# Strassen-Winograd gate and up products: one trace order for all sets, with P4 cut into two halves

## The chip, the cores and the metric

The kernel runs on 1 core of one Trainium2 chip. The metric is the device time of one execution in microseconds (us), and the time of a kernel is the median of several executions. All values are float32; the products are made from float32r halves, as told below.

## The reference, cut to what matters

One step of a decoder layer for 512 prompt rows plus 8 sample rows, with a width of 2048. The part that the change touches is the first half of the SwiGLU feed-forward layer: `silu(h1 @ w_gate) * (h1 @ w_up)`, with `h1` of 520 rows by 2048, and `w_gate` and `w_up` of 2048 by 5632. Before it come attention, pooling, an output projection and a layer norm; after it `w_down` and a second layer norm.

```
a = silu(einsum('btd,df->btf', h1, w_gate)) * einsum('btd,df->btf', h1, w_up)
ff = einsum('btf,fd->btd', a, w_down)
h = layer_norm(alpha*h1 + ff, ...)
```

## The kernel before, in words

**Tiling.** The 5632 output columns are 44 tiles of 128, taken as 22 pairs. For each pair there is a gate set `g<i>` and an up set `u<i>` (class `Set`), which run in turn: g0, u0, g1, u1, g2 and so on; pairs 5 and 16 come last. A set multiplies a 2x2 block of weights (two column tiles by two halves of the 2048 inputs) by a 2x2 block of activations (two halves of the inputs by two halves of 260 rows) by the Strassen-Winograd scheme: seven products P1 to P7 in place of eight.

**A product** (`prod`, line 969) takes 128x1024 weights: a raw block `q(r, c)` as loaded for P1, P2 and P4, or a sum of raw blocks, made by DVE on a 128x1024 tile (`weight_sum`, line 196), for P7, P6, P5 and P3. The sums chain: P7's goes into P6's, P6's overwrites the same block, and that goes into P5's and P3's. The weights are then split in two halves of 512 columns (`split`): ACT rounds them to float32r (`wh`, the CAST of line 187) and DVE subtracts to get the rest (`wl`, line 188). Each half feeds 12 matmuls of 128x260: four times `wh` by high part (L203), `wh` by low part (L204), `wl` by high part (L206). So a product is 24 matmuls.

**Rings.** `wh` and `wl` come from rings of `WB` = 5 slots, dealt out in the order in which the code is traced. The cast into a slot waits until the matmuls of the split five places earlier in the trace have read it. Raw blocks (512 KB each, loads of line 180 on SP's queue) lie in a ring of six, four blocks to a set.

**Banks.** Three PSUM banks per set: `al` (named `p1_...`) takes P1, P6, P5 and P3 in turn, accumulating, and between them the parts `c21`, `c22` are read out of it; `ga` (`p7_...`) takes P7 and, after its copy to `c22`, P4; `de` (`p2_...`) takes P2 alone. P5 may not write `al` until `c21` is read from it after P6 (line 1038, or line 1036 where P1 is filled in). P3 may not write it until `c22` is read from it after P5 (line 1050).

**Which sets have what.** g0 and u0 have P1 and P2 made ahead (`ahead`), so they run five products. Ten up sets (u1 to u4, u6 to u11) have P1 made ahead ("filled"): six products. All others run seven.

**The order.** `run` (line 1007) traces the products; the tile framework then schedules every engine's instructions by its own model, so a matmul may stand earlier or later than traced, as far as data, ring and bank allow. PE, ACT, DVE and SP each execute their list strictly in that order. Work that rides along: after each up set `staged` makes sums and splits of the result (lines 1097 to 1112) and stores them to `t_d`, pulled forward by `next(side)` in the next gate set.

Of the kernel before, what the change touches and what calls it, by code (L numbers as in the profile page):

```python
# [67 lines left out]
def hybrid_step(ctx, tc, xin, w_in, w_o, w_g, w_u, w_d, w_pool, par_d, cst_d, ident_d, ln2gb, kct_d, vc_d, hist_d,  # L68
# [83 lines left out]
    def row_tile(name, w=NTOK):  # L152

        return ap_.tile([P, NTOK], F32, tag="row", name=name, bufs=bufs["row"])[:, :w]
# [28 lines left out]
    def split(s, name, lo=None):  # L183

        wh, wl = [sp[0].tile(list(s.shape), F32R, tag=t, bufs=sp[1]) for t in ("wh", "wl")]
        with tc.high_priority(prio[0]):
            nc.scalar.copy(wh, s)  # L187
            last_lo[0] = (lo or nc.vector).tensor_sub(wl, s, wh.bitcast(F32)).ins  # L188
        return wh, wl
# [10 lines left out]
    def products(out, wh, wl, hi, lo, first, last, onto=False):  # L200

        for j, o in enumerate(out):
            nc.tensor.matmul(o, wh, hi[j], start=first, stop=False, skip_group_check=onto)  # L203
            nc.tensor.matmul(o, wh, lo[j], start=False, stop=False, skip_group_check=onto)  # L204
        for j, o in enumerate(out):
            nc.tensor.matmul(o, wl, hi[j], start=False, stop=last, skip_group_check=onto)  # L206
# [48 lines left out]
    with ExitStack() as sa:  # L255
# [185 lines left out]
        for h in range(2):  # L441
            for g in range(4):
                n = h * 4 + g + 1
# [244 lines left out]
        def sample_attention():  # L688
# [10 lines left out]
            nc.scalar.copy(sT.rearrange("p j n -> p (j n)"), st_.rearrange("p j t b -> p (j t b)"))  # L699
            prod = pa.tile([P, 8, NS], F32, tag="smp", name="prod")  # L700
            nc.vector.tensor_add(prod, qd[:, 0], qd[:, 1])
            for i in range(2):
                ts = slice(4 * i, 4 * i + 4)
# [111 lines left out]
    def bank(name, w=HN):  # L815
        return ps.tile([P, 512], F32, tag="bank", name=name, bufs=banks)[:, :w]
# [130 lines left out]
    class Set:  # L947
# [18 lines left out]
            self.s((1, 0), (0, 0), (1, 0), nc.vector.tensor_sub)  # L966
            self.s3 = True

        def prod(self, n, bk, first=True):


            b = {1: "b11", 2: "b21", 3: "b22", 4: "t4", 5: "t1", 6: "t2", 7: "t3"}[n]
            src = {1: lambda: self.q(0, 0), 2: lambda: self.q(0, 1), 4: lambda: self.q(1, 1),
                   7: lambda: self.q(1, 0) if self.s3 else self.s((1, 0), (0, 0), (1, 0), nc.vector.tensor_sub),
                   6: lambda: self.s((1, 0), (1, 1), (1, 0), nc.vector.tensor_sub),
                   5: lambda: self.s((0, 0), (1, 0), (0, 0), nc.vector.tensor_add),
                   3: lambda: self.s((0, 1), (0, 1), (1, 0), nc.vector.tensor_sub)}[n]()
            for g in range(2):
                wh, wl = split(src[:, g * 512:(g + 1) * 512], f"{self.name}_{n}{g}")
                if g == 0 and n == 1:  # L980
                    self.early()
                if g == 0 and n == 3 and self.next and (self.next.p1 is not None or self.next.bk):

                    self.next.early()
                for kk in range(4):
                    k = 4 * g + kk
                    sl = slice(kk * P, (kk + 1) * P)
                    hi, lo = bop[b][k // 2]
                    products([bk], wh[:, sl], wl[:, sl], [hi[:, k % 2, :]], [lo[:, k % 2, :]], k == 0 and first, k == 7, True)
# [17 lines left out]
        def run(self, c11, c12, c21, c22, side=(), out=None):  # L1007

            side = iter(side)
            r = row_tile(f"p_{self.name}")  # L1010
            filled = self.p1 is not None
            al, de = [self.bk.get(n) for n in (1, 2)]
            if not filled:
                self.p1 = r[:, HALF[0]]
                if al is None:
                    al = bank(f"p1_{self.name}")
                    self.prod(1, al)
                nc.scalar.copy(self.p1, al)
            else:
                al = bank(f"p1_{self.name}")  # L1020
            ga = bank(f"p7_{self.name}")
            next(side, None)
            self.prod(7, ga)
            next(side, None)
            kept = de is not None
            if filled and not kept:
                de = bank(f"p2_{self.name}")
                self.prod(2, de)
            if filled:
                nc.vector.tensor_add(c22, ga, self.p1)  # L1030
            else:
                nc.scalar.copy(c22, ga)
            self.prod(6, al, filled)
            next(side, None)
            if filled:
                nc.vector.tensor_add(c21, al, self.p1)
            else:
                nc.scalar.copy(c21, al)
            if filled or kept:
                self.prod(4, ga, False)  # L1040
            else:
                de = bank(f"p2_{self.name}")
                self.prod(2, de)
            next(side, None)
            nc.vector.tensor_add(c11, de, self.p1)
            if out:
                out(0)
            self.prod(5, al, False)
            next(side, None)
            nc.vector.tensor_add(c22, c22, al)  # L1050
            if not (filled or kept):
                self.prod(4, ga, False)
            next(side, None)
            nc.vector.tensor_add(c21, c21, ga)
            if out:
                out(1)
            self.prod(3, al, False)
            if filled:
                nc.vector.tensor_add(c12, al, self.p1)
                return c12  # L1060
            return al
# [68 lines left out]
    for j, s in enumerate(sets[NKEEP + 1::2][:NFILL]):  # L1130
        if j % 2 == 0:
            f = pb.tile([P, 2, HN], F32, tag="fill", name=f"fill{j}", bufs=NF)
# [82 lines left out]
    def column_pair(c, j):  # L1215

        A = {(r, b): wd[c, j, r, b] for r in range(2) for b in range(2)}
        tri = ps.tile([P, 3, 512], F32, tag="tri", name=f"tri{c}_{j}", bufs=2)[:, :, :HN]
        ga, de, al = [tri[:, i, :] for i in range(3)]
        ac = acc4[j]  # L1220
        if c == 0:
            for r in range(2):
                h = ac[:, 2 * r:2 * r + 2, :]
                nc.scalar.activation(h, h, AF.Copy, scale=ALPHA)

        def prod(n, bk, src, first=True):
            wh, wl = split(src, f"d{c}_{j}_{n}")
            for k in range(KP):
                hi, lo = ops[c][n][k][:, 0, :], ops[c][n][k][:, 1, :]
                products([bk], wh[:, k, :], wl[:, k, :], [hi], [lo], k == 0 and first, k == KP - 1, True)  # L1230

        def add(t, a, b, op):
            weight_sum(op, A[t], A[a], A[b])
            return A[t]


        prod(1, al, A[0, 0])
        yield
        prod(7, ga, add((1, 0), (0, 0), (1, 0), nc.vector.tensor_sub))
        nc.vector.tensor_add(ac[:, 1:3, :], ac[:, 1:3, :], tri[:, 0::2, :])  # L1240
        yield
        prod(2, de, A[0, 1])
        yield
        prod(6, al, add((1, 0), (1, 1), (1, 0), nc.vector.tensor_sub), False)
        nc.vector.tensor_add(ac[:, 0, :], ac[:, 0, :], al)
        yield
        prod(4, ga, A[1, 1], False)
        yield
        prod(5, al, add((0, 0), (1, 0), (0, 0), nc.vector.tensor_add), False)
        nc.vector.tensor_add(ac[:, 0:2, :], ac[:, 0:2, :], tri[:, 0::2, :])  # L1250
        yield
        prod(3, al, add((0, 1), (0, 1), (1, 0), nc.vector.tensor_sub), False)
        nc.vector.tensor_add(ac[:, 2:4, :], ac[:, 2:4, :], tri[:, 1:3, :])
        yield
# [9 lines left out]
    g, before = [column_pair(0, j) for j in range(2)]  # L1264
# [5 lines left out]
    for x, (c, j) in enumerate(pairs[2:], 2):  # L1270
        g = column_pair(c, j)
# [4 lines left out]
        for i in range(5):  # L1276
# [7 lines left out]
            elif j < 2 * len(PLAIN) and i == 0:  # L1284
# [3 lines left out]
                f = j  # L1288
# [233 lines left out]
```

## Time and profile before

| | |
|---|---|
| time, median of 3 | 1931.59 us (1929.88 to 1933.46) |
| span of the profiled execution | 1931.1 us, 0.5 under the median; its own time is not listed apart |
| PE busy (matmul) / PEld (weight load) | 1894.4 us (98%) / 1865.8 us (97%) |
| DVE busy / ACT busy | 1539.9 us (80%) / 944.1 us (49%) |
| DMA queue 1 | 315.71 MB, 49.7% of 16 engines |
| mean granted TensorE clock | 0.992 |

The gate and up sets run from about 590 to 1448 us of the span. In a timeline row the columns are start, duration, engine, line, operation, output and inputs, shapes, count; brackets at the end give the idle time just before, by the modelled end of the work before it, and what ended it.

### The profile page before, as it was taken

What the parts mean: (1) busy time and instruction counts of PE and PEld (TensorE: products, weight loads), DVE (VectorE), ACT (ScalarE), POOL (GpSimd) and SP (SyncE); (2) the same over time, 40 slices, a digit from 0 to 9 for tenths busy, and PEclk for the clock granted to TensorE, in tenths of its full rate; (3) what the DMA queues carried; (4) which work ended last, traced back from release to release, by engine and by line L of the source; (5) the groups of instructions that cost most, each with busy time, mean ns of one, the idle gap of its engine ahead of it and who ended that gap; (6) DMA issues with size and microseconds to landing.
All of it is one profiled execution on the core that took longest, in us unless ns stands there. A gap on an engine that the chain in (4) does not pass through costs nothing.

```text
span 1931.1 us, 39334 instructions
## 1 busy us (share of the span) xinstructions
PE 1894.4 (98%) x15533; PEld 1865.8 (97%) x15533; DVE 1539.9 (80%) x2734; ACT 944.1 (49%) x1808; POOL 2.7 (0%) x9
## 2 busy tenths in 40 slices
PE   9999999999999999999999999999999999999996
PEld 8999999999989999999999999999999999999996
DVE  6666667768777888888888888888877888888878
ACT  6644445545654544554455555555554444344341
POOL 0000000000000000000000000000000000000000
PEclk9999999999999999999999999999999999999998
DMA  8732222665744555454545445454469664645332
GB/s 276 233 101 66 71 78 75 211 202 193 250 150 164 160 160 172 142 162 158 175 139 178 141 138 165 146 167 145 164 212 356 214 221 162 223 163 202 94 99 89
DMA packets 145241, 319.28 MB, mean 165 GB/s; under 512 B 14288, under 2 KB 66232, under 8 KB 144952
## 3 DMA queue, kind: packets, MB, share of 16 engines
q1 hardware_dynamic: 144480, 315.71, 49.7%
q8 instruction: 122, 2.00, 0.4%
q10 hardware_dynamic: 576, 1.05, 0.2%
q14 instruction: 63, 0.52, 0.1%
HBM read 265.22 MB, written 54.03 MB: 165 GB/s over the span
## 4 chain that ended last, share of the span: by engine, by line
PE 92%; DVE 4%; ACT 2%; DMA 1%; issue 1%; SPq 0%; DVEq 0%; ACTq 0%
PE p_g L203 7%; PE p_g L204 7%; PE p_g L206 7%; PE p_u L203 7%; PE p_u L206 7%; PE p_u L204 7%; PE tri L203 7%; PE tri L206 7%; PE tri L204 7%; PE o L203 3%; PE o L206 3%; PE o L204 3%; PE p_u L996 2%; PE mm_u L203 2%; PE mm_u L206 2%; PE mm_u L204 2%
## 5 line engine op out<-in xcount | busy, mean ns | idle before, releaser
L187 ACT CAST rr<-fr 128x512 fp32r<-128x512 f32 (+1 forms) x1056 | 658.0, 643 | 776.6 <-DVE fr L196 224.0
L188 DVE TENSOR_TENSOR rr<-fr,rr 128x512 fp32r<-128x512 f32 (+1 forms) x1056 | 738.0, 717 | 264.5 <-ACT rr L187 253.2
L196 DVE TENSOR_TENSOR fr<-fr 128x1024 f32<-128x1024 f32 (+1 forms) x304 | 319.7, 1052 | 5.8 <-DMA fr<-in_w_g_dram 5.0
L203 PE MATMUL p_g<-rr 128*128 128x260 f32 x830 | 235.5, 285 | 7.4 <-ACT rr L187 7.1
L206 PE MATMUL p_g<-rr 128*128 128x260 f32 x830 | 230.6, 282 | 0.0
L204 PE MATMUL p_g<-rr 128*128 128x260 f32 x788 | 221.8, 282 | 0.0
L203 PE MATMUL p_u<-rr 128*128 128x260 f32 x770 | 217.5, 283 | 0.2 <-ACT rr L187 0.2
L206 PE MATMUL p_u<-rr 128*128 128x260 f32 x770 | 215.3, 282 | 0.0
L204 PE MATMUL p_u<-rr 128*128 128x260 f32 x748 | 210.6, 282 | 0.0
L206 PE MATMUL tri<-rr 128*128 128x260 f32 x696 | 196.8, 283 | 1.5 <-DVE rr L188 1.5
L203 PE MATMUL tri<-rr 128*128 128x260 f32 x696 | 197.0, 283 | 0.7 <-ACT rr L187 0.7
L204 PE MATMUL tri<-rr 128*128 128x260 f32 x696 | 196.7, 283 | 0.0
L203 PEld LDWEIGHTS p_g<-rr 128*128 128x128 f32 x830 | 156.2, 188 | 9.9 <-ACT rr L187 9.4
L206 PEld LDWEIGHTS p_g<-rr 128*128 128x128 f32 x830 | 155.2, 189 | 0.0
L204 PEld LDWEIGHTS p_g<-rr 128*128 128x128 f32 x788 | 148.1, 188 | 0.0
L203 PE MATMUL o<-rr 128*128 128x260 f32 x512 | 145.0, 284 | 0.3 <-ACT rr L187 0.3
L203 PEld LDWEIGHTS p_u<-rr 128*128 128x128 f32 x770 | 144.9, 188 | 0.3 <-ACT rr L187 0.3
L206 PEld LDWEIGHTS p_u<-rr 128*128 128x128 f32 x770 | 144.6, 189 | 0.0
L204 PE MATMUL o<-rr 128*128 128x260 f32 x512 | 144.1, 282 | 0.0
L206 PE MATMUL o<-rr 128*128 128x260 f32 x512 | 143.6, 282 | 0.2 <-DVE rr L188 0.2
L204 PEld LDWEIGHTS p_u<-rr 128*128 128x128 f32 x748 | 140.6, 188 | 0.0
L206 PEld LDWEIGHTS tri<-rr 128*128 128x128 f32 x696 | 131.3, 189 | 2.2 <-DVE rr L188 2.2
(320 smaller groups left out, 4570.0 us busy)
## 6 DMA issues: line engine op xcount, KB each, us to landing
fr<-in_w_u_dram SPq DMA_DIRECT2D x100, 512.0 KB
fr<-in_w_g_dram SPq DMA_DIRECT2D x90, 512.0 KB
fr<-in_w_d_dram SPq DMA_DIRECT2D x64, 640.0 KB
t_d<-fr SPq DMA_DIRECT2D x140, 260.0 KB
fr<-in_w_o_dram SPq DMA_DIRECT2D x64, 512.0 KB
fr<-in_w_in_dram SPq DMA_DIRECT2D x48, 512.0 KB
rr<-t_d SPq DMA_DIRECT2D x87, 260.0 KB
mid_b<-t_d SPq DMA_DIRECT2D x53, 260.0 KB
```

The source lines that it names most:

```text
L187: nc.scalar.copy(wh, s)
L188: last_lo[0] = (lo or nc.vector).tensor_sub(wl, s, wh.bitcast(F32)).ins
L196: i = op(*args).ins
L203: nc.tensor.matmul(o, wh, hi[j], start=first, stop=False, skip_group_check=onto)
L204: nc.tensor.matmul(o, wh, lo[j], start=False, stop=False, skip_group_check=onto)
L206: nc.tensor.matmul(o, wl, hi[j], start=False, stop=last, skip_group_check=onto)
L996: nc.tensor.matmul(bk, self.q(0, n - 1)[:, k * P:(k + 1) * P], z1[0][4 * (n - 1) + k // 2][:, k % 2, :], start=(k == 0), stop=(k == 7))
```

## The change

Before, the order of tracing depended on the set: P7, P2, P6, P4, P5, P3 where P1 is filled; P7, P6, P4, P5, P3 in g0 and u0; P1, P7, P6, P2, P5, P4, P3 in all others. Now each set traces [P1], P7, [P2], P6, first half of P4, P5, second half of P4, P3. With P4 in two traced halves, its two splits also take their ring slots at two places, before and behind P5's.

```diff
-        def prod(self, n, bk, first=True):
+        def prod(self, n, bk, first=True, halves=(0, 1)):
...
-            for g in range(2):
+            for g in halves:
                 wh, wl = split(src[:, g * 512:(g + 1) * 512], f"{self.name}_{n}{g}")
...
             next(side, None)
             self.prod(7, ga)
             next(side, None)
-            kept = de is not None
-            if filled and not kept:
+            if de is None:
                 de = bank(f"p2_{self.name}")
                 self.prod(2, de)
...
-            if filled or kept:
-                self.prod(4, ga, False)
-            else:
-                de = bank(f"p2_{self.name}")
-                self.prod(2, de)
+            self.prod(4, ga, False, (0,))
             next(side, None)
             nc.vector.tensor_add(c11, de, self.p1)
             if out:
                 out(0)
             self.prod(5, al, False)
             next(side, None)
             nc.vector.tensor_add(c22, c22, al)
-            if not (filled or kept):
-                self.prod(4, ga, False)
+            self.prod(4, ga, False, (1,))
             next(side, None)
             nc.vector.tensor_add(c21, c21, ga)
             if out:
                 out(1)
             self.prod(3, al, False)
```

Lines of the changed kernel that the orders below and the prediction name: 1040 is `c11` (1045 before), 1045 is `c22` (1050 before), 1048 is the sum into `c21` (1054 before), 1037 the copy of `c21` (1038 before), 1061 to 1063 the Silu of the gate (1067 to 1069 before), 1105 a staged cast (1111 before).

First place, PE's order in g6 where P6 ends, before (`p1_g6` is `al`, `p7_g6` is `ga`):

```order
L206 MATMUL p1_g6_8279<-rr_61 128x260
L203 MATMUL p1_g6_8279<-rr_61 128x260
L204 MATMUL p1_g6_8279<-rr_61 128x260
L206 MATMUL p1_g6_8279<-rr_61 128x260
L203 MATMUL p7_g6_8312<-rr_61 128x260 [waits Activation_49]
L204 MATMUL p7_g6_8312<-rr_61 128x260
L203 MATMUL p1_g6_8279<-rr_61 128x260 [waits Activation_49]
L204 MATMUL p1_g6_8279<-rr_61 128x260
L206 MATMUL p1_g6_8279<-rr_61 128x260 [waits DVE_49]
```

And now, PE's order in g6 at the end of the first half of P4:

```order
L204 MATMUL p7_g6_8312<-rr_61 128x260
L206 MATMUL p7_g6_8312<-rr_61 128x260
L203 MATMUL p7_g6_8312<-rr_61 128x260 [waits Activation_49]
L204 MATMUL p7_g6_8312<-rr_61 128x260
L203 MATMUL p1_g6_8279<-rr_61 128x260 [waits Activation_49]
L204 MATMUL p1_g6_8279<-rr_61 128x260
L206 MATMUL p1_g6_8279<-rr_61 128x260 [waits DVE_49]
```

Before, two matmuls of P4 followed the last of P6, and P5 followed them. Now twelve matmuls of P4, its whole first half, stand between P6 and the first pair of the second half, and P5 starts after that pair.

Second place, PE's order at the seam from g6 to the filled set u6, before:

```order
L204 MATMUL p7_g6_8312<-rr_61 128x260
L206 MATMUL p7_g6_8312<-rr_61 128x260
L203 MATMUL p7_u6_8518<-mid_b_3870,rr_61 128x260 [waits Activation_49]
L204 MATMUL p7_u6_8518<-mid_b_3870,rr_61 128x260
L203 MATMUL p1_g6_8279<-rr_61 128x260 [waits DVE_49]
```

And now:

```order
L204 MATMUL p7_g6_8312<-rr_61 128x260
L206 MATMUL p7_g6_8312<-rr_61 128x260
L203 MATMUL p7_u6_8518<-mid_b_3870,rr_61 128x260 [waits Activation_49]
L204 MATMUL p7_u6_8518<-mid_b_3870,rr_61 128x260
L203 MATMUL p2_u6_8547<-mid_b_3870,rr_61 128x260
L204 MATMUL p2_u6_8547<-mid_b_3870,rr_61 128x260
L203 MATMUL p1_g6_8279<-rr_61 128x260 [waits DVE_49]
```

A pair of u6's P2 has moved ahead of g6's P3, beside the pair of u6's P7 that stood there. In both, P4's last rows run just ahead of the seam.

Third place, ACT's order at the same seam, before (the cast that waits for DVE and PE is u6's P7, first half; the one behind it P7, second half; the one that waits for a DMA is u6's P2, first half):

```order
L187 CAST rr_61<-fr_60 128x512 [waits PE_49,Activation_49]
L187 CAST rr_61<-fr_60 128x512 [waits DVE_49,PE_49,Activation_49]
L187 CAST rr_61<-fr_60 128x512 [waits PE_49,Activation_49]
L187 CAST rr_61<-fr_60 128x512 [waits DMAHW3_49,PE_49]
L187 CAST rr_61<-fr_60 128x512 [waits PE_49,Activation_49]
```

And now (the cast that waits for a DMA and PE is u6's P2, first half; the two behind it are P7's halves):

```order
L187 CAST rr_61<-fr_60 128x512 [waits DVE_49,Activation_49]
L187 CAST rr_61<-fr_60 128x512 [waits PE_49,Activation_49]
L187 CAST rr_61<-fr_60 128x512 [waits DMAHW2_49,PE_49,Activation_49]
L187 CAST rr_61<-fr_60 128x512 [waits DVE_49]
L187 CAST rr_61<-fr_60 128x512
L1062 ACTIVATE fr_60<-fr_60 128x520 [waits DVE_49]
```

The cast of u6's P2 has moved ahead of both casts of u6's P7. In the trace's ring order P2's first half has the slot five places behind the second half of g6's P4.

## The prediction

> **What bounds the kernel now.** I read the page first, then the waits of PE, busy time by stretches, and the timelines of PE, ACT and DVE around PE's waits.
>
> ```profile
> PE 1894.4 (98%) x15533; PEld 1865.8 (97%) x15533; DVE 1539.9 (80%) x2734; ACT 944.1 (49%) x1808; POOL 2.7 (0%) x9
> ```
>
> PE is busy for 98% of the span, and the change keeps the number of its matmuls. So only waits of PE can move the time. Its waits, longest first:
>
> ```profile
> PE p_g L203 <- ACT rr L187: 7.1, 11, 0.6
> ...
> PE tri L203 <- DVE fr L1240: 0.8, 1, 0.8
> ...
> PE p_g L203 <- ACT fr L1038: 0.3, 1, 0.3
> ...
> PE p_u L203 <- ACT rr L187: 0.2, 1, 0.2
> ```
>
> Of these, the rows of `p_g` and `p_u` lie in the gate and up sets: twelve short waits for the cast of a weight half, and one for the copy of `c21`. By stretches (us, then PE, PEld, DVE, ACT, POOL, clock, DMA):
>
> ```profile
> 790.00:990.00 200.00, 196.62 (x1626) 195.41 (x1626) 172.53 (x279) 99.79 (x188) 0.00 (x0) 1.00 0.51 162
> 1190.00:1450.00 260.00, 259.26 (x2162) 259.05 (x2162) 216.40 (x332) 139.29 (x261) 0.00 (x0) 1.00 0.50 166
> ```
>
> The waits belong to the first half, where a seven-product gate set is followed by a filled up set. In the second, where all sets run seven products, PE hardly waits (0.74 of 260 us): there is nothing to win there. One wait in detail, on PE and then on ACT:
>
> ```profile
> 708.31 0.28 PE L203 MATMUL p_g<-rr 128*128 128x260 f32 x1
> 708.43 0.28 PE L204 MATMUL p_g<-rr 128*128 128x260 f32 x1
> 708.54 0.28 PE L206 MATMUL p_g<-rr 128*128 128x260 f32 x1
> 709.47 0.39 PE L203 MATMUL p_g<-rr 128*128 128x260 f32 x1 [0.64 <-ACT rr L187]
> 709.70 0.28 PE L204 MATMUL p_g<-rr 128*128 128x260 f32 x1
> 709.81 0.32 PE L203 MATMUL p_g<-rr 128*128 128x260 f32 x1
> 709.97 0.28 PE L204 MATMUL p_g<-rr 128*128 128x260 f32 x1
> ```
> ```profile
> 708.80 0.62 ACT L187 CAST rr<-fr 128x512 fp32r<-128x512 f32 x1 [0.81 <-PE p_g L204]
> 709.32 0.37 ACT L1038 COPY fr<-p_g 128x260 f32<-128x260 f32 x1
> 709.59 0.62 ACT L187 CAST rr<-fr 128x512 fp32r<-128x512 f32 x1
> ```
>
> Matmuls start 0.12 apart. The last L204 of P6 starts at 708.43; 0.37 later ACT, idle for 0.81 before, casts P4's first half, and 0.05 after that cast's end PE goes on. The cast waited for a slot: traced P6, P2, P5, P4, the first half of P4 is the fifth split behind the second half of P6, but PE runs P2 before P6 and a pair of P4 right behind P6. So P4's slot comes free only when its weights are due. The start gap is 0.93 in place of 0.12, and the next two uneven steps are 0.23 and 0.16: 0.81 + 0.11 + 0.04 = 0.96 us for a wait.
>
> **What goes.** Ten of the eleven waits of `p_g` are of this form. In the first, P5's pair waits once more, for the copy of `c21`:
>
> ```profile
> 631.31 0.28 PE L206 MATMUL p_g<-rr 128*128 128x260 f32 x1
> 632.23 0.39 PE L203 MATMUL p_g<-rr 128*128 128x260 f32 x1 [0.64 <-ACT rr L187]
> 632.46 0.28 PE L204 MATMUL p_g<-rr 128*128 128x260 f32 x1
> 633.04 0.39 PE L203 MATMUL p_g<-rr 128*128 128x260 f32 x1 [0.29 <-ACT fr L1038]
> 633.26 0.28 PE L204 MATMUL p_g<-rr 128*128 128x260 f32 x1
> ```
>
> From 631.31 to 633.26 are 1.95 us in place of four steps, 0.48: 1.47. Now P2 is traced before P6, as PE runs it, and twelve matmuls of P4 (1.44 us) lie between P6 and the next accumulation into `al`; the copy of 0.37 fits under them. Counting five splits back, P4's halves use slots that P7 and P6 left at least 25 matmuls (3 us) before. So all eleven should go: 10 x 0.96 + 1.47 = 11.1 us.
>
> **What comes.** At the seam to a filled up set (second and third place of the orders) PE ends P4's second half and goes to pairs of the next set's P7 and P2. P2's first half has the slot of P4's second half, whose last L204 runs one row before the seam, and ACT has that cast ahead of P7's. So the pair of P7, whose own weights are long summed, waits for two casts. What two take in a row, after a wait of the first:
>
> ```profile
> 833.38 1.14 ACT L187 CAST rr<-fr 128x512 fp32r<-128x512 f32 x2 [3.61 <-DMA fr<-in_w_u_dram]
> ```
>
> From the slot's last L204: 0.37 + 1.14 + 0.05 = 1.56 us to the pair, which would stand 0.24 behind that L204. That is 1.32, and with the uneven restart (0.11 + 0.04) 1.47 us. The orders show it at nine seams: those into u2 to u4 and u6 to u11, and not into u1. 9 x 1.47 = 13.2 us. P3, P2 and all that stands behind move by as much; nothing runs meanwhile on PE.
>
> One more comes at the end. In u16 no next set's P1 lies between P5 and P3, and P4's second half is scheduled ahead of P5, so P3 follows P5 at once and waits for `c22`. The nearest row is PE's wait for a DVE addition in the down stage:
>
> ```profile
> 1479.18 0.28 PE L206 MATMUL tri<-mid_b,rr 128*128 128x260 f32 x1
> 1480.25 0.39 PE L203 MATMUL tri<-mid_b,rr 128*128 128x260 f32 x1 [0.79 <-DVE fr L1240]
> ```
> ```profile
> 1479.50 0.70 DVE L1240 TENSOR_TENSOR fr<-fr,tri 128x520 f32<-128x520 f32 x1 [0.22 <-PE tri L206]
> ```
>
> DVE starts 0.32 after the last matmul's start, and PE 0.05 after DVE's end. With an addition of 0.42 (row at 708.57 below) that is 0.79, less the usual 0.12, plus the restart: 0.8 us.
>
> **What is only just hidden.** Two covers are thin. First, `c22` before P3 elsewhere: the order now has 14 matmuls of the next set's P1 between P5 and P3, where it had some 26 before. DVE's queue there holds a subtraction, the next set's sum and then `c22`. The rows:
>
> ```profile
> 697.22 0.62 ACT L187 CAST rr<-fr 128x512 fp32r<-128x512 f32 x1 [2.11 <-PE p_g L204]
> ```
> ```profile
> 697.87 0.69 DVE L188 TENSOR_TENSOR rr<-fr,rr 128x512 fp32r<-128x512 f32 x1 [1.35 <-ACT rr L187]
> ...
> 706.23 0.68 DVE L188 TENSOR_TENSOR rr<-fr,rr 128x512 fp32r<-128x512 f32 x1
> 706.83 1.22 DVE L196 TENSOR_TENSOR fr<-fr 128x1024 f32<-128x1024 f32 x1
> 707.97 0.68 DVE L188 TENSOR_TENSOR rr<-fr,rr 128x512 fp32r<-128x512 f32 x1
> 708.57 0.42 DVE L1045 TENSOR_TENSOR fr<-p_g,fr 128x260 f32<-128x260 f32 x1
> ```
>
> From the L204 that frees the slot: 0.37 to the cast, 0.65 to the subtraction, 0.60 to the sum, 1.14 to the addition, 0.42 for it, 0.05 to PE: 3.23 us. P3 starts 28 matmuls behind that L204: 3.36. So about 0.1 us is left at some thirty seams. I take no wait there; each 0.1 us short would cost 3 us in all. Nothing can be gained there, since PE did not wait before.
>
> Second, the raw block of the filled set's P2 takes the place of the one that P5 has just split. Asking and landing in the trace, slowest and fastest of eight:
>
> ```profile
> 826.63 0.45 SPq L180 DMA_DIRECT2D fr<-in_w_u_dram  x1
> ```
> ```profile
> 903.73 0.45 SPq L180 DMA_DIRECT2D fr<-in_w_u_dram  x1
> ```
> ```profile
> 909.16 0.62 ACT L187 CAST rr<-fr 128x512 fp32r<-128x512 f32 x1 [2.29 <-DMA fr<-in_w_u_dram]
> ```
>
> From 826.63 to the cast at 833.38 are 6.75 us, from 903.73 to 909.16 5.43. Now the load can be asked for some 2.7 us after P2's end (0.3 for the last matmul, some 0.6 of queued DVE work, `c11`, two subtractions at 0.60, 0.2 of issue), and the slot is free 71 matmuls, 8.5 us, plus 0.37 after P2's end: 6.2 us for the load. It comes between 0.8 early and 0.6 late. I take nothing for it, being in the middle; late by 0.6 each time it would cost 5 us.
>
> SP's queue carries the same loads and stores; P2's load stands ahead of P6's in all sets now, and both land well before they are due in the seven-product sets (one product more is between them and their casts). The down stage has the same matmuls in the same order.
>
> **The sum.** -11.1 + 13.2 + 0.8 = +2.9 us. On the profiled span of 1931.1 that is 1934.0; its median lies 0.5 above, so 1934.5 us. A difference under 0.2% (3.9 us) is about what a measurement of this kernel can't tell from none, so this is "no change", on the slow side.
>
> **The rivals.**
>
> *The wait goes and none comes* (0.08). For it: tracing P2, P6, P4, P5, P4, P3 makes the ring's order that in which PE runs them, in all sets. Against it: the ACT and PE orders at the seam. It gives 1931.6 - 11.1 = 1920.5.
>
> *The new wait has one cast's price* (0.10), if P7's cast runs while the slot is still taken and only P2's comes behind it. 9 x 0.96 + 0.8 - 11.1 = -1.7: 1929.9. Against it: ACT in the row at 833.38 stood idle for 3.61 us with a second cast behind the waiting one.
>
> *The load of P2's weights becomes the wait at the seam* (0.12). P7's cast stands behind P2's on ACT, so a late load now stops PE, where before it stopped only ACT (3.61 us idle at 833.38, PE going on). It decides where a load takes over 6.2 us; at the slowest row's 6.75 at each of nine seams 5 us more: 1939.5, slower.
>
> *P3 waits for `c22` at all thirty seams* (0.09). At 0.2 us each 6 us more: 1940.5, slower. For it: 0.1 us of cover. Against it: these durations vary by 0.01.
>
> *The clock drops* (0.06). The trace has a stretch in which PE's longest wait was 1.28 us, and in the next the granted clock was 0.53:
>
> ```profile
> 48.10:51.50 3.40, 1.97 (x12) 1.06 (x10) 1.13 (x6) 2.54 (x4) 0.00 (x0) 1.00 0.25 87
> 51.50:54.90 3.40, 3.26 (x15) 3.25 (x15) 3.00 (x5) 2.31 (x6) 0.00 (x0) 0.53 0.29 97
> ```
> ```profile
> 49.52 0.30 PE L366 MATMUL xt<-fr,mid_a 128*128 128x128 f32 x1 [1.28 <-DVE fr L372]
> ```
>
> A wait of 1.47 us leaves PE 1.9 of 3.4 us, near the 1.97 of that stretch. If each such stretch brought one at half clock, it would cost 1.7 us; with some five of nine waits wholly inside one, 9 us: 1943. Against it: PE loads weights for 1.06 us of that stretch, and would for 1.9 here, and waits of 0.96 left the clock at 1.00 from 790 to 990. [...]
>
> **How the numbers follow.** The forecast has 0.55; its own range is 1932.5 to 1937. The range, 1929.5 to 1941, takes in the one-cast case, late loads and the short cover of P3, and leaves out the clock and the case without a wait. Within 0.2%: 0.40 of the forecast's 0.55, the one-cast case, 0.02 of the others: 0.52. Slower: 0.15 + 0.12 + 0.07 + 0.06 = 0.40. Faster: 0.08.
>
> **What would show it.** In the waits of PE the eleven rows of `p_g` on L187 are gone; nine of `p_u` on L187 stand in their place, each with an idle time near 1.2 us where 0.64 stood, at the first row of a P7, with two casts in a row before it on ACT. The stretch from 1190 to 1450 stays near 259 us busy. The prediction is wrong if those waits are absent, if ACT's wait before the two casts ends on a DMA and not on PE, if `p_g` or `p_u` waits for L1045 more than once, or if the clock in the stage is under 1.00.

## The result and the profile after

| | before | after |
|---|---|---|
| median (range), 20 runs each | 1931.75 us (1929.4 to 1934.07) | 1934.95 us (1932.51 to 1939.31) |
| span of the profiled execution | 1931.1 us | 1934.8 us |
| stage: first L203 row of `p_g` on `rr` to first row of `tri` | 593.9 to 1449.4: 855.5 us | 594.5 to 1452.4: 857.9 us |

The ratio is 1.0018, with a 95% interval of 1.0012 to 1.0024 (2.3 to 4.6 us): 3.2 us slower, where 2.9 were forecast on top of the median.

The page's busy times after, and PE's waits in the order of their length:

```profile
PE 1893.6 (98%) x15533; PEld 1863.0 (96%) x15533; DVE 1535.7 (79%) x2734; ACT 939.7 (49%) x1808; POOL 2.7 (0%) x9
```
```profile
PE p_u L203 <- ACT rr L187: 10.5, 9, 1.3
...
PE p_u L203 <- DVE fr L1045: 0.6, 1, 0.6
```

PE does the same work. The eleven waits of `p_g` for a cast and the one for the copy are gone; nine of `p_u` stand in their place, and one of `p_u` for `c22`. By stretches (us, then PE, PEld, DVE, ACT, POOL, clock, DMA share, GB/s):

```profile
790.00:990.00 200.00, 192.95 (x1599) 191.71 (x1598) 172.47 (x278) 99.07 (x185) 0.00 (x0) 1.00 0.49 161
1190.00:1450.00 260.00, 259.09 (x2159) 258.49 (x2158) 212.33 (x330) 136.23 (x261) 0.00 (x0) 1.00 0.49 165
```

PE idles 7.1 of 200 us where there was 3.4, and the second half, where no filled sets run, is as full as it was. The clock is 1.00 in both. One of the nine, on PE and on ACT:

```profile
830.01 0.28 PE L204 MATMUL p_g<-rr 128*128 128x260 f32 x1
830.12 0.28 PE L206 MATMUL p_g<-rr 128*128 128x260 f32 x1
831.56 0.39 PE L203 MATMUL p_u<-mid_b,rr 128*128 128x260 f32 x1 [1.15 <-ACT rr L187]
831.78 0.28 PE L204 MATMUL p_u<-mid_b,rr 128*128 128x260 f32 x1
```
```profile
830.37 1.66 ACT L187 CAST rr<-fr 128x512 fp32r<-128x512 f32 x3 [2.56 <-PE p_g L204]
```

ACT is idle for 2.56 us, until the L204 at 830.01 has read the slot, and 0.36 behind that row it casts three halves in a row. The first is P2's. The second, P7's, is the one PE needs; by the step of two casts (1.14) it ends at 831.51, and PE goes on at 831.56. The gap is 1.44 in place of 0.12, and the next step 0.22. Eight of the nine are alike (1.31 and 0.11); the one into u8 is 0.13 longer. Together 8 x 1.42 + 1.55 = 12.9 us. The wait in u16:

```profile
1447.62 0.28 PE L206 MATMUL p_u<-rr 128*128 128x260 f32 x1
1448.51 0.36 PE L203 MATMUL p_u<-rr 128*128 128x260 f32 x1 [0.61 <-DVE fr L1045]
1448.71 0.28 PE L204 MATMUL p_u<-rr 128*128 128x260 f32 x1
```

0.89 and 0.20 in place of twice 0.12: 0.85 us.

### The profile page after: what moved, and what is told of

Same layout as the page of the kernel before. It is cut to its first block, busy times and chain, and to the rows that moved or that the text cites. A ratio compares the mean times of both kernels' runs of the same rounds, so it can differ in the third digit from the quotient of the medians.

```text
span 1934.8 us, 39143 instructions
## 1 busy us (share of the span) xinstructions
PE 1893.6 (98%) x15533; PEld 1863.0 (96%) x15533; DVE 1535.7 (79%) x2734; ACT 939.7 (49%) x1808; POOL 2.7 (0%) x9
## 4 chain that ended last, share of the span: by engine, by line
PE 91%; DVE 3%; ACT 2%; DMA 2%; issue 1%; SPq 0%; DVEq 0%; ACTq 0%
PE p_g L203 7%; PE p_g L204 7%; PE p_g L206 7%; PE p_u L203 7%; PE p_u L206 7%; PE p_u L204 7%; PE tri L203 6%; PE tri L206 6%; PE tri L204 6%; PE o L203 3%; PE o L206 3%; PE o L204 3%; PE p_u L996 2%; PE mm_u L203 2%; PE mm_u L206 2%; PE mm_q L203 2%
## 5 line engine op out<-in xcount | busy, mean ns | idle before, releaser
L196 DVE TENSOR_TENSOR fr<-fr 128x1024 f32<-128x1024 f32 (+1 forms) x304 | 319.3, 1050 | 5.4 <-DMA fr<-in_w_g_dram 5.0
L203 PE MATMUL p_g<-rr 128*128 128x260 f32 x830 | 234.5, 283 | 0.0
L204 PE MATMUL p_g<-rr 128*128 128x260 f32 x788 | 221.8, 282 | 0.0
L203 PE MATMUL p_u<-rr 128*128 128x260 f32 x770 | 218.2, 283 | 0.6 <-DVE fr L1045 0.6
L204 PE MATMUL p_u<-rr 128*128 128x260 f32 x748 | 210.9, 282 | 0.0
L203 PE MATMUL tri<-rr 128*128 128x260 f32 x696 | 197.1, 283 | 0.8 <-ACT rr L187 0.8
L204 PE MATMUL tri<-rr 128*128 128x260 f32 x696 | 196.7, 283 | 0.0
L203 PEld LDWEIGHTS p_g<-rr 128*128 128x128 f32 x830 | 156.1, 188 | 0.0
L204 PEld LDWEIGHTS p_g<-rr 128*128 128x128 f32 x788 | 148.1, 188 | 0.0
L203 PEld LDWEIGHTS p_u<-rr 128*128 128x128 f32 x770 | 144.7, 188 | 0.8 <-ACT rr L187 0.8
L203 PE MATMUL o<-rr 128*128 128x260 f32 x512 | 145.0, 284 | 0.3 <-ACT rr L187 0.3
L204 PE MATMUL o<-rr 128*128 128x260 f32 x512 | 144.0, 282 | 0.0
L204 PEld LDWEIGHTS p_u<-rr 128*128 128x128 f32 x748 | 140.7, 188 | 0.0
```

The costliest lines, as they stand in the source:

```text
L196: i = op(*args).ins
```

## The experiments

The profile names a cast as what ends the nine waits. That leaves open why the cast is late: because ACT has another one ahead of it (theory A), because five slots are too few for this order, whichever cast goes first (B), or because the load of P2's weights ends last (C). The kernel before was timed beside each: its median was 1932.08 us beside the first three runs below and P4 whole, and 1931.80 us beside the other four.

**One cast held back.** The changed kernel; in the up sets the cast of P2's first half may not stand ahead of P7's on ACT.

```diff
-            nc.scalar.copy(wh, s)
+            last_cast[0] = nc.scalar.copy(wh, s).ins
...
+                behind = last_cast[0]
                 wh, wl = split(src[:, g * 512:(g + 1) * 512], f"{self.name}_{n}{g}")
+                if n == 2 and g == 0 and self.name[0] == "u":
+                    tc.add_manual_dep(last_cast[0], behind.name, ...NoSync...)
```

> Theory A (ACT's order): the nine waits of 1.43 us at the seams exist only because ACT has the cast of P2's first half ahead of P7's two casts. With that one cast held behind P7's (only in the up sets) PE's order stays and every cast at the seam has its slot long before it is due: the nine p_u rows on ACT go, 12.9 us less than the changed kernel, 1922.0 us, about 9.7 under the kernel before. Theory B (the ring of five slots is too short for this order): the wait moves to the next product's cast, the nine waits stay in another place, 1934.9 +- 1.5. Theory C (the load of P2's weights is what comes last at the seam): with P7's casts free the wait becomes one of P2's pair and of ACT on a DMA, some 0.1 to 0.6 us at each seam, 1923 to 1927.

Measured: 1922.63 us, 0.9950 of before (0.9938 to 0.9963). PE's waits of `p_u`:

```profile
PE p_u L203 <- DVE fr L1049: 0.6, 1, 0.6
PE p_u L203 <- ACT rr L187: 0.6, 2, 0.4
```

The nine are gone, and two short ones (0.2 and 0.4) are left. The stage, by the first starts of the two groups:

```profile
L203 PE MATMUL p_g<-rr x830: 277/283/289, 589.5 to 1414.4; 128*128 128x260 f32 x166
```
```profile
L203 PE MATMUL tri<-rr x696: 277/283/388, 1435.0 to 1846.0; 128*128 128x260 f32 x174
```

From 589.5 to 1435.0 are 845.5 us, 12.4 less than in the changed kernel; the medians differ by 12.3. That speaks for A, and against B and C: the five slots and the loads are as they were. PE's order, which had been expected to stay, moved a little: the pair of P2 that stood behind P7's pair at the seam now stands behind P3. But the row that waited was P7's, ahead of that pair. So the new waits cost what their rows say, and they come from the place of one cast in ACT's queue.

**The kernel before, casts in turn.** The same idea on the kernel before: each cast of the gate and up sets behind the one traced before it.

```diff
-            nc.scalar.copy(wh, s)
+            i = nc.scalar.copy(wh, s).ins
+            if in_turn[0]:
+                if last_cast[0] is not None:
+                    tc.add_manual_dep(i, last_cast[0].name, ...NoSync...)
+                last_cast[0] = i
```

> The kernel before, with every cast of the gate and up sets on ACT kept in the order of the trace. Theory A: the eleven waits of p_g on ACT go, since P4's first half no longer gets the slot that PE has only just left; 11.1 us less than before, 1920.7 us. Theory B (five slots are too few for PE's order, P2 ahead of P6, whatever ACT's order): the waits stay or move to P6's or P2's pairs, 1930 to 1933. Either way it tells what the change's first half (the waits of 0.96 and 1.47 gone) was worth without the change's new order.

Measured: 1920.57 us, 0.9944 of before (0.9931 to 0.9956), 11.5 us less. The stretch of the waits now, and the one wait of PE in a gate or up set that is listed:

```profile
790.00:990.00 200.00, 200.00 (x1670) 200.00 (x1669) 178.13 (x288) 101.07 (x191) 0.00 (x0) 1.00 0.48 160
```
```profile
PE p_u L212 <- DVE rr L193: 0.2, 1, 0.2
```

PE is busy for all of the 200 us. So the first term of the prediction, -11.1, was worth 11.5 by itself, and could be had without the change. But holding ACT to the order of the trace altered more than ACT's queue, as the copy of `c21` (after P6) and the addition of `c11` (after P2) show:

```profile
703.40 0.38 ACT L1044 COPY fr<-p_g 128x260 f32<-128x260 f32 x1 [0.34 <-PE p_g L212]
```
```profile
706.21 0.42 DVE L1051 TENSOR_TENSOR fr<-p_g,fr 128x260 f32<-128x260 f32 x1
```

The copy now comes 2.8 us ahead of the addition; in the kernel before it came behind it (709.32 and 708.57). PE has gone back to P6 ahead of P2, and P2's 24 matmuls lie between P6 and P5. Theory B was about PE's order with P2 ahead of P6, and that order is gone, so this run does not part A from B for the old waits. Its median is the lowest of all that were run; by the intervals it can't be told from the first experiment's.

**P2's move alone.** P2 ahead of P6 in all sets, P4 whole and where it was.

```diff
-            if filled and not kept:
+            if not kept:
...
-            else:
-                de = bank(f"p2_{self.name}")
-                self.prod(2, de)
```

> One part of the change alone: P2 traced ahead of P6 in all sets, P4 whole behind P5 in the unfilled ones as before. The eleven p_g waits on ACT should go (-11.1). What the halving of P4 is for should show: P3 stands one matmul behind P5 at eleven seams of unfilled sets and waits for the addition into c22, 0.85 us each as at the end of u16 in the changed kernel, +9.4, and eleven matmuls behind it at the other nine, where the addition of about 1.0 us fits under 1.3: nothing. At the seams into the filled up sets P2's slot is left twelve matmuls before its pair, not two: 1.68 - 1.44 + 0.11, about 0.3 us in ten places, +3, and 1.4 once at the seam into u1. Sum against before +2.7: 1934.5 us (1931 to 1937). Rival: c22's addition stands behind other work on DVE and costs 1.5 us and more in all twenty places: over 1950.

Measured: 1935.36 us, 1.0014 of before (1.0006 to 1.0023), +3.3. PE's waits, and the addition at one of twelve places in the sets without P1 filled in:

```profile
PE p_u L203 <- ACT rr L187: 8.4, 13, 1.2
...
PE p_g L203 <- ACT rr L187: 0.6, 1, 0.6
PE p_u L203 <- DVE fr L1047: 0.6, 1, 0.6
```
```profile
1036.42 0.42 DVE L1047 TENSOR_TENSOR fr<-fr,p_u 128x260 f32<-128x260 f32 x1 [0.21 <-PE p_u L206]
```

The eleven old waits are gone with this half of the change. In their place PE stops every 41.1 us from 1036 to 1406, each time for a gap of 0.89, and twice more: once with `p_g`, at 1427.74, and once in u16, where `c22`'s addition is named. At 1036 a cast ends 0.08 behind the addition and gets the name. The addition it is all the same: at all twelve places it ends 0.15 ahead of PE's row, as it does in u16 of the changed kernel, and the wait was forecast there for P3 one matmul behind P5. So P2's move takes the 11.1 us away and gives 12 x 0.85 = 10.2 back. The halving is there for this. The small waits expected at the ten seams into filled sets (3 us) did not come, but some 3 us of uneven ones elsewhere; the one of 1.4 into u1 did.

**The halving alone.** P4 in halves in all sets, P2 where it was.

```diff
-            if filled or kept:
-                self.prod(4, ga, False)
-            else:
+            if not (filled or kept):
                 de = bank(f"p2_{self.name}")
                 self.prod(2, de)
+            self.prod(4, ga, False, (0,))
...
-            if not (filled or kept):
-                self.prod(4, ga, False)
+            self.prod(4, ga, False, (1,))
```

> The other part of the change alone: P4 in halves around P5 in all sets, but P2 traced where it stood before, behind P6 in the unfilled sets. Theory A: the ring is dealt so that neither P4's nor P2's first cast gets a slot that PE has only just left (at the seam the slot is left fourteen matmuls before, 1.68 us, and two casts in a row take 1.56 with 0.12 more): the eleven waits of p_g go, and no wait of 1.43 comes. P3 stands three matmuls behind P5 at the ten seams into filled sets: 0.72 us each, 7.2. Against the kernel before -11.1 + 7.2: 1928 us, and up to 3 more if two casts at fourteen matmuls are only just late. Rival: the halving is what makes the seam wait of the changed kernel, 1.43 at nine seams or more and the eleven waits stay or go: 1934 to 1946.

Measured: 1926.63 us, 0.9972 of before (0.9962 to 0.9983), 5.2 less. All of `p_g`'s waits, and one of the places:

```profile
PE p_g L203 <- DVE fr L1049: 2.8, 10, 0.3
```
```profile
788.17 0.28 PE L203 MATMUL p_u<-mid_b,rr 128*128 128x260 f32 x1
788.29 0.28 PE L204 MATMUL p_u<-mid_b,rr 128*128 128x260 f32 x1
788.85 0.39 PE L203 MATMUL p_g<-rr 128*128 128x260 f32 x1 [0.28 <-DVE fr L1049]
789.07 0.28 PE L204 MATMUL p_g<-rr 128*128 128x260 f32 x1
```

No wait for a cast is left, old or new. Ten waits for `c22` came as forecast, at 0.44 + 0.10 = 0.54 and not 0.72; 11.1 - 5.4 = 5.7, near the 5.2. So either half of the change takes the old waits away. Why no wait comes at the seam is seen in ACT's casts there:

```profile
786.86 0.62 ACT L187 CAST rr<-fr 128x512 fp32r<-128x512 f32 x1 [1.71 <-PE p_g L204]
788.30 0.62 ACT L187 CAST rr<-fr 128x512 fp32r<-128x512 f32 x1 [0.82 <-PE p_g L204]
...
790.69 1.14 ACT L187 CAST rr<-fr 128x512 fp32r<-128x512 f32 x2 [1.23 <-DMA fr<-in_w_u_dram]
```

The cast at 786.86 ends 0.69 before the pair of P7 at 788.17, which runs on time; the one that waits for a load of up weights, P2's, comes two casts later, at 790.69, and nobody waits for it. Here the scheduler put P2's cast behind P7's by itself, so the halving does not bring the seam's wait. P5, and not P4, ends just ahead of this seam (`c22`'s addition follows at once), so P2's slot was also left earlier; which of the two kept the wait away, this run alone does not say.

**P4 whole, ahead of P5.** The changed kernel without halves.

```diff
-            self.prod(4, ga, False, (0,))
+            self.prod(4, ga, False)
...
-            self.prod(4, ga, False, (1,))
```

> The same order in all sets, but P4 whole ahead of P5, not halved around it. P2's first half then has the slot of P5's second half, which PE again runs last before the seam: the wait of 1.43 us stands at ten seams (into u1 too) instead of nine, and P3 behind it finds c22 summed meanwhile. Theory A: changed kernel + 1.4 = 1936.4 us, p_u on ACT ten times, no more than one row on the addition into c22. Rival (the halves of P4 are what makes the wait, by leaving P4's slot last): no wait at the seams, 1922.

Measured: 1970.62 us, 1.0198 of before (1.0184 to 1.0212). Both expectations were wrong. PE's waits, and one seam on PE, ACT and SP's queue:

```profile
PE p_u L203 <- ACT rr L187: 29.8, 10, 3.5
```
```profile
852.09 0.28 PE L206 MATMUL p_g<-rr 128*128 128x260 f32 x1
855.44 0.58 PE L203 MATMUL p_u<-mid_b,rr 128*128 128x260 f32 x1 [3.07 <-ACT rr L187]
```
```profile
854.25 1.66 ACT L187 CAST rr<-fr 128x512 fp32r<-128x512 f32 x3 [4.26 <-DMA fr<-in_w_u_dram]
```
```profile
848.05 1.75 SPq L180 DMA_DIRECT2D fr<-in_w_u_dram  x2
```

The ten waits are there, but ACT's idle time ends on a DMA: the two loads that SP issues from 848.05 to 849.80 bring P2's block, and its cast, again ahead of P7's, can't start before 854.25. This is the prediction's rival of the late load, in a kernel where it holds. A second loss shows in the stretches:

```profile
852.00:855.40 3.40, 0.37 (x4) 0.16 (x2) 1.33 (x3) 1.15 (x3) 0.00 (x0) 0.98 0.93 342
855.40:858.80 3.40, 3.36 (x16) 3.36 (x17) 1.40 (x3) 1.05 (x2) 0.00 (x0) 0.52 0.17 66
```

After nine of the ten gaps of 2.90 to 3.76 us the clock is halved, five times for 3.4 us as here, and four times for 6.8 us that begin inside the gap. PE's steps are 0.22 then in place of 0.12, and the steps that come late behind the ten gaps sum to 18.6 us. The gaps themselves sum to 31.4 above the steps, 19.5 more than the changed kernel's nine, whose late steps sum to 1.0. That is 37.1 us in all; the stage took 896.5 us in the profiled execution, 38.6 more than the changed kernel's, and the medians differ by 35.7.

**The same with the one cast held back.** P4 whole ahead of P5, with the added lines of the first experiment.

> P4 whole ahead of P5 in all sets, as in the run that took 1970.6 us, but with the cast of P2's first half behind P7's two on ACT. Theory A (that run's waits near 3.3 us are P7's casts queued behind one that waits for the load of P2's weights): the ten waits go; the load may still land late, but P2's pair is due only some 48 matmuls (5.8 us) behind the seam. What is left is P3 three matmuls behind P5 at ten seams, waiting for the addition into c22: the chain is 0.97 us as at the end of u16, less 0.36, with the restart 0.72 each: 1922.6 + 7.2 = 1930 us (1927 to 1933). Theory B (the load itself comes too late for PE in this order): the waits move to P2's pair, still over 1950.

Measured: 1932.55 us, 1.0002 of before (0.9993 to 1.0011). Holding the cast back was worth 38 us in this order, load and clock included: the load is asked for as late as before (some 4 us ahead of the seam in both), but P2's own pair has time. The number lies in the expected range, but the rest came otherwise than told: no wait is for `c22` except in u16. PE's waits, and the worst seam on PE and DVE:

```profile
PE p_u L203 <- ACT rr L187: 5.4, 10, 1.8
```
```profile
674.49 0.28 PE L206 MATMUL p_g<-rr 128*128 128x260 f32 x1
676.54 0.39 PE L203 MATMUL p_u<-mid_b,rr 128*128 128x260 f32 x1 [1.77 <-ACT rr L187]
```
```profile
672.99 0.70 DVE L1109 TENSOR_TENSOR fr<-fr 128x520 fp32r<-128x520 f32 x1 [1.84 <-DMA t_d<-fr]
...
674.54 1.22 DVE L196 TENSOR_TENSOR fr<-fr 128x1024 f32<-128x1024 f32 x1
```

P7's cast at 675.87 follows the sum of L196, and that stood on DVE behind a staged subtraction that waits 1.84 us for a store to finish. The addition into `c22` is done meanwhile. It is the same pattern on another engine: an instruction that waits holds up one that PE needs. The gaps vary from 0.44 to 2.05.

**The cover of `c22`.** The changed kernel with this addition in two parts, then in four (the edit for four; the other has two slices).

```diff
-            nc.vector.tensor_add(c22, c22, al)
+            for x in range(0, HN, HN // 4):
+                nc.vector.tensor_add(c22[:, x:x + HN // 4], c22[:, x:x + HN // 4], al[:, x:x + HN // 4])
```

> The changed kernel with the addition into c22 ahead of P3 made in two halves of 130 columns. The prediction called the cover of this addition thin, 0.1 us; the trace after shows PE's row 0.12 to 0.16 us behind the addition's end. A half costs some 0.07 to 0.15 more (0.42 at 260 columns and 0.69 at 520 leave 0.15 that does not shrink). So 34 places lose between nothing and 0.1 us each: 1935 to 1938 us. Rival (the cover is thick, the chain ends well before P3): 1935.0, the same as the run with quarters.

> The same in four quarters of 65 columns, which lengthens the chain by 0.2 to 0.45 us. Thin cover: it shows at 34 places with 0.06 to 0.31 us and some 0.1 of restart each, 6 to 14 us more than the changed kernel: 1941 to 1949 us, and PE waits of p_g and p_u for this line. Thick cover: 1935.0 as with one addition.

Measured: 1938.58 us (1.0038 of before, 1.0025 to 1.0050) and 1945.18 us (1.0070, 1.0057 to 1.0082). The addition in the changed kernel, in halves and in quarters, in the same gate set (rows of three kernels):

```profile
1105.96 0.42 DVE L1045 TENSOR_TENSOR fr<-fr,p_g 128x260 f32<-128x260 f32 x1
```
```profile
1105.18 0.48 DVE L1046 TENSOR_TENSOR fr<-fr,p_g 128x130 f32<-128x130 f32 x2
```
```profile
1106.98 0.61 DVE L1046 TENSOR_TENSOR fr<-fr,p_g 128x65 f32<-128x65 f32 x4
```

P3's first row starts at 1106.59 in the changed kernel, 0.21 behind the addition's end, of which DVE to PE takes 0.05 by the prediction's row at 1480.25 (0.15 in u16): 0.16 of cover, as in nine gate sets; in twenty up sets the row starts 0.165 behind, 0.11 of cover. Two parts last 0.06 longer. No P3 is listed as waiting except in u16, but in the up sets the step behind P3's first row grows:

```profile
1085.60 0.34 PE L203 MATMUL p_u<-rr 128*128 128x260 f32 x1
1085.78 0.28 PE L204 MATMUL p_u<-rr 128*128 128x260 f32 x1
```

That is 0.18 in place of 0.12, with the row 0.10 behind the addition's end: 1.2 us in twenty up sets. In the gate sets, with 0.15 left, the step is 0.13. Four parts last 0.19 longer, and then PE stumbles at P3 itself:

```profile
1107.49 0.28 PE L204 MATMUL p_u<-mid_b,rr 128*128 128x260 f32 x1
1107.65 0.39 PE L203 MATMUL p_g<-rr 128*128 128x260 f32 x1
1107.87 0.29 PE L204 MATMUL p_g<-rr 128*128 128x260 f32 x1
```

0.16 and 0.22 in place of 0.12: 0.14 here and 0.18 in the up sets, some 5.3 us at 31 places. So what could be spared was less than 0.06 in the up sets, and about that in the gate sets. In halves the time rose by 3.6 (1935 to 1938 was expected), and not by the 1.2 alone: in u16 DVE's order put other work between the two halves, and that wait grew from 0.61 to 2.14; a wait for `c21`'s addition near 650 us adds 0.5. In quarters it grew to 2.27, and the clock was halved behind it for 3.4 us; with the 5.3 these two are most of the 10.2 us over the changed kernel.

## Why the prediction was right, point by point

- **What goes, 11.1 us.** Right. The eleven rows are gone, and the kernel before without them, though with another order on PE, is 11.5 us faster.
- **What comes, nine waits of 1.47 us.** Right in number, place, form and order on ACT: two casts, P2's first, behind P4's last L204. They measured 1.42 each, since the restart costs 0.11 and the further uneven step of 0.04 does not come: 12.9 us in place of 13.2. Holding one cast back took 12.3 off.
- **u16, 0.8 us.** 0.85; PE came 0.15 behind the addition's end, where 0.05 was reckoned.
- **Sum, +2.9.** The measured terms give -11.1 + 12.9 + 0.85 = 2.7. The median rose by 3.2, the stage in the profiled executions by 2.4. The prediction called a difference under 0.2% one that can't be told from none; the measured one, 2.3 to 4.6 us, can.
- **Cover of `c22`, 0.1 us.** 0.11 in the up sets and 0.16 in nine gate sets, counted as the prediction did. No wait there, as taken; by the run in halves still less could be spared.
- **P2's load, 0.8 early to 0.6 late.** It was taken as nothing because it lay in the middle, so that it came out so was partly luck. Its 0.2 of issue was the author's estimate: in the profile after, SP issues this load at 824.25, 0.03 behind the end of the subtractions. By the landings in the trace the nine loads took 4.5 to 5.5 us from the issue. Eight landed in time; the one into u8 landed at 869.21, 0.10 ahead of the cast at 869.31, which fits the 0.13 more there, though the row names PE. What a late load does in that place the run with P4 whole showed.
- **Rivals.** No wait came at one cast's price, since P7's cast never ran while the slot was taken. The clock stayed at 1.00 behind all nine.

What the prediction did not say: the old waits and the new ones are alike. Slots are dealt in the order of the trace, while PE and ACT run in another, so a cast comes due when PE has only just left its slot. In the new waits that cast stands ahead of one that could run; in the old ones PE's next pair needs that cast itself. Both kernels lose some 11 to 13 us by it, so the change swapped one for the other. The kernel before with its casts in turn, and the changed kernel with one cast held back, lose almost none of it; for the old waits it stays open whether ACT's queue or PE's order is what matters.

## What to carry to other kernels

Where buffers are dealt in trace order and an engine runs its queue strictly in order, look at both orders at once: the nine waits here, 12.9 us together, arose where an instruction whose slot came last stood ahead of one that was due first, and with P4 whole it was the load that came last. Before reordering the work of the busy engine, try pinning the order of the helper's queue at that one place; here one pinned cast was worth 12.3 us, and the reordering without it cost 3.2. Look afterwards at what else the scheduler moved. Where P3-like steps follow close behind an accumulation, measure the cover before the chain grows: 0.11 us, counted as the prediction did, was enough here, and 0.06 more of chain already showed at twenty places.

## What the runs showed of the hardware

**The granted clock and short gaps.** The nine gaps of 1.43 to 1.57 us left the clock at 1.00. In the run with P4 whole nine of ten gaps of 2.90 to 3.76 were followed by a stretch at half clock, and one of 2.93 was not:

```profile
893.80:897.20 3.40, 0.79 (x7) 0.58 (x5) 1.83 (x4) 1.15 (x3) 0.00 (x0) 1.00 0.95 324
897.20:900.60 3.40, 3.36 (x28) 3.37 (x29) 1.96 (x4) 1.67 (x3) 0.00 (x0) 1.00 0.30 118
```

The single gap of 2.05 us of the run with P4 whole and the cast held back did bring one:

```profile
677.20:680.60 3.40, 3.40 (x18) 3.40 (x17) 1.93 (x5) 1.71 (x3) 0.00 (x0) 0.50 0.55 176
```

In u16 the gap of 2.55 of the run in quarters brought one too, and the gap of 2.42 of the run in halves did not. So the length of the gap alone does not decide. In the clock that the trace of P4 whole has on record, the nine stretches last 3.41 us (five) or 6.83 us (four), and they start 13, 25, 38, 50, 63, 87, 100 and 112 steps of 3.413 us behind the first, wherever the gaps lie.

So 2.05 us, 1.77 of it idle, was enough in one run, and 2.93 was not in another. Laid on steps of that length, the 2.05 puts 1.77 of idle time into one step and the 2.93 at most 1.64; but the 2.42 without a stretch at half clock puts 1.79 into one. So the idle time in one step does not decide alone either, and what does was not shown.

**What a short addition costs.** The addition into `c22` on DVE took 0.42 us with 260 columns, 0.48 in two of 130 together and 0.61 in four of 65 together: about 0.06 for each cut.
